# Sparse attention stage of a two-layer trunk: TensorE's order written out, attention as a three-step pipeline, index scores out of PSUM by ScalarE

## The chip, the core and the metric

The kernel runs on one NeuronCore of a Trainium2 chip. The core has five engines, each with its own in-order instruction queue: TensorE (PE, matrix products into PSUM; its weight loads are listed apart as PEld), VectorE (DVE), ScalarE (ACT), GpSimd (POOL) and SyncE (SP), which here only issues DMAs. Engines meet through semaphores. The metric is the device time of one execution in microseconds (us); the kernel before takes 1209.16 us, the median of three runs (1204.34 to 1213.13).

## The reference

A trunk of two layers on 512 tokens of width 1024. Layer 0 mixes tokens by sparse attention whose keys an indexer chooses, layer 1 by a gated linear attention; beside either, four heads attend to 256 memory rows. Each layer ends in a mixture of 32 experts. What the change touches lies wholly in layer 0's mixer:

```python
def dsa_mixer(x, cos, sin, w_in, idx_k_g, idx_k_b):
    q, k, v, qi, ki, wi, qm = _split(x @ w_in, DSA_SPLITS)   # 768 768 768 512 64 8 256
    q, k, qi = (rope of each, 12, 12 and 8 heads of 64)
    ki = apply_rope(layer_norm(ki, idx_k_g, idx_k_b), cos, sin)
    wi = wi * (IDX_HEADS ** -0.5 * IDX_DIM ** -0.5)
    out = sparse_attention(q, k, v, qi, ki, wi, topk)        # topk = 128
    return out.reshape(B, S, SEQ_WIDTH), qm

def block(args):                                             # of sparse_attention
    rel = jax.nn.relu(jnp.einsum('bqhd,bsd->bqhs', qib, ki))
    score = jnp.einsum('bqhs,bqh->bqs', rel, wib)            # 8 index heads, weighted
    score = jnp.where(causal[None], score, -jnp.inf)
    _, sel = lax.top_k(score, topk)
    ...                                                      # softmax over the chosen keys, times v
```

`memory_attention` is a plain softmax attention of the 256 columns `qm` over keys and values `mem @ w_kv`.

## The kernel before

Tokens lie in four blocks of 128 partitions (`NT` = 4). A projection of f32 accuracy is made of three fast matmuls (`mm3`, L340 to L342): each operand is split into a high part (L295, ScalarE) and the rest (L296, VectorE). `in_proj` (L558) makes one projection of 384 columns: for each token block 8 x 3 matmuls into one of two PSUM buffers (`mm`), then what `consume` does with the result. For keys and queries that is `rope` (ScalarE copies the result out, L467; VectorE multiplies, L452 and L455; GpSimd adds, L456), later three transposes by TensorE (L463) and a copy; for values a copy alone. Keys, queries and values come in two halves of six heads, in the order keys, queries, values.

**The indexer** (L594): for the query blocks 1 to 3 (block 0 needs no choice), eight heads' scores over 256, 384 or 512 keys. Each head is one matmul (L606) into one of two PSUM buffers (`sc`); VectorE takes it out with relu and the head's weight in one operation (L609 for head 0, L612 for the others), and GpSimd adds it to the sum (L613). Then 16 steps choose 8 keys each: MAX8 (L621) and MATCH_REPLACE (L622) on VectorE; at the end a mask is written (L624). The function is a generator: each head and each step of the choice is one `yield`.

**Attention** (`attend`, L527): a generator with one `yield` for a query block of a pair of heads. It holds two scores (L535), the softmax of both (`softmax_rows`: mask-add with row maximum L497, or the maximum alone L501 for memory, negation L503, exp on ScalarE L504, reciprocal L506, scaling L507), transposes (L463) with copies by ScalarE (L467) and the products with the values (L545), two heads of 64 columns side by side. There are 8 such items for memory and 24 for the six pairs of heads, with one to four key blocks. `put_mixed` (L515) splits a finished pair for the output projection.

**What sets the order.** `dsa_layer` draws steps from these generators between the token blocks of the projections: `KVC` steps of the indexer between the parts of the memory keys, and by `IS` so many steps of indexer, memory attention and `early` (the first three pairs of heads) after each token block. The scheduler of the framework may then reorder instructions of each engine, TensorE's too: it places each by when its inputs are expected. The last three pairs run between the parts of the second layer's memory keys (`mem_kv(1)`). Weights are loaded by SP's DMAs; `clear` writes zeros to the experts' output from a GpSimd memset, by DMAs in ScalarE's queue.

Of the kernel before, what the change touches and what calls it, by code (L numbers as in the profile page):

```python
# [40 lines left out]
KVC = 6  # L41
IS = ((6, 0, 0), (7, 0, 0), (5, 1, 0), (0, 1, 0), (0, 0, 1), (0, 0, 2))
# [177 lines left out]

def run(steps, n=None):

    r = None
    for r in itertools.islice(steps, n):
        pass
    return r


class Trunk:
# [105 lines left out]
    def mm3(self, ps, a, b):  # L335

        for k in range(KD):
# [4 lines left out]
            self.nc.tensor.matmul(ps, al, bh, start=False, stop=(k == KD - 1))  # L342

# [126 lines left out]
    def mem_kv(self, layer):  # L470
# [5 lines left out]
        for half, dst in enumerate((kmT, vm)):  # L476
            w = self.split_pieces(wv[:, :, half * 256:(half + 1) * 256], 256)
            a, b = (m, w) if half else (w, m)
            for j in range(2):
                ps = self.mm([P, 512])  # L480
                self.mm3(ps[:, :NMEM], lambda k: self.piece(a, k, j * P, (j + 1) * P), lambda k: self.piece(b, k))
# [36 lines left out]
    def attend_start(self):  # L518
        self.pr, self.pt = Ring(self.ar, 512, 3), Ring(self.ar, 512, 4)
# [30 lines left out]

    def mem_attention(self, qmT, kmT, vm, mix):
# [6 lines left out]
    def in_proj(self, wview, c0, n, x, consume, between=None, w=None, lags=(LAG,) * NT):  # L558
        w = w or self.split_pieces(wview[:, :, c0:c0 + n], n)
        for i in range(NT):  # L560
            ps = self.mm([P, 512])
            self.mm3(ps[:, :n], lambda k: self.piece(x, k, i * P, (i + 1) * P), lambda k: self.piece(w, k))
# [31 lines left out]
    def indexer(self, qiT, kiT, wi, bias, acc_b):  # L594

        nc = self.nc
# [3 lines left out]
        for i in range(1, NT):  # L600
            n = (i + 1) * P
            acc = acc_b.v(n, at=(0, 0, 2, 5)[i] * P)
            for h in range(IDX_H):
                j, s = divmod(h, 2)
                ps = self.sc([P, 512])
                nc.tensor.matmul(ps[:, :n], qiT[s * HD:(s + 1) * HD, j, i * P:(i + 1) * P],  # L606
                                 kiT[s * HD:(s + 1) * HD, :n], start=True, stop=True)
# [7 lines left out]
            nc.gpsimd.tensor_scalar(acc, acc, 0.0, 1.0, op0=OP.add, op1=OP.mult)  # L615
# [19 lines left out]
    def dsa_layer(self, Y):  # L635
# [85 lines left out]
        for kv_b, kmT, vm in self.mem_kv(0):  # L721
            run(choice, KVC)
# [1086 lines left out]
```

## Time and profile before

| | us |
|---|---|
| median of three runs | 1209.16 |
| lowest, highest | 1204.34, 1213.13 |
| profiled execution | 1212.06 |
| its span, first to last instruction | 1210.3 |
| TensorE busy in the span | 1105.9 |
| VectorE, ScalarE busy | 591.2, 398.5 |

The mean granted TensorE clock is 0.939 of full speed. The sparse attention stage fills about the first 330 us; behind it come the output projection with a layer norm and the router, to about 405, and the first experts' stage, to about 650; the second layer has the rest. A busy time is an average over stages with different limits, so the rows below are of single stretches. The clock column (PEclk) is the mean of the granted clock over a window: 1.00 is the higher of its two levels, 0.50 the lower.

### The profile page before, as it was taken

The numbers are of one execution on the slowest core, as the hardware profiler recorded it, in microseconds if no ns is written. First come the engines' busy times: TensorE is split into PE (matmuls) and PEld (weight loads), VectorE is DVE, ScalarE is ACT, GpSimd is POOL, SyncE is SP. The second block draws the span as 40 slices with busy tenths as digits, with TensorE's granted clock in tenths as the row PEclk, the third lists the DMA queues.
The fourth block names the chain that finished last, engine by engine and source line by source line (L and its number), as shares of the span: only waits on it lengthen the run. The fifth ranks groups of instructions, "written<-read, shape, count | busy, mean of one in ns | idle before, by whom it ended". The sixth has DMA issues, their size and how long they took to land. (4 is left out here: it accounts for less than half of the span.)

```text
span 1210.3 us, 20344 instructions
## 1 busy us (share of the span) xinstructions
PE 1105.9 (91%) x7864; PEld 799.5 (66%) x7864; DVE 591.2 (49%) x1601; ACT 398.5 (33%) x853; POOL 178.8 (15%) x179
## 2 busy tenths in 40 slices
PE   7999999999998899888988999899896999888985
PEld 7866887767697656444444778899896666444442
DVE  6778894555647422114116745992737322114125
ACT  6421343556512222112215534453501222112212
POOL 0425201000002021111000000553001111111000
PEclk9988899999998899998899999899997999998988
DMA  9033410341577699999997202137196899999992
GB/s 320 27 105 109 131 40 14 101 145 32 189 289 270 253 395 419 422 366 384 396 407 257 79 22 80 41 117 267 65 413 243 317 400 397 368 368 392 408 410 109
DMA packets 101509, 289.35 MB, mean 239 GB/s; under 512 B 13948, under 2 KB 43021, under 8 KB 89762
## 3 DMA queue, kind: packets, MB, share of 16 engines
q1 hardware_dynamic: 88704, 257.42, 56.4%
q0 software_dynamic: 9792, 20.00, 4.5%
q10 hardware_dynamic: 2914, 10.61, 2.2%
q8 instruction: 63, 1.03, 0.4%
q14 instruction: 36, 0.29, 0.1%
HBM read 272.19 MB, written 31.46 MB: 251 GB/s over the span
## 5 line engine op out<-in xcount | busy, mean ns | idle before, releaser
L1103 PE MATMUL mm<-blk,blk 128*64 128x256 f32 x2048 | 246.8, 391 | 30.9 <-DMA blk<-in_w 28.9
L340 PE MATMUL mm<-blk,blk 128*128 128x256 f32 (+2 forms) x800 | 262.7, 329 | 4.6 <-ACT blk L467 3.6
L341 PE MATMUL mm<-blk,blk 128*128 128x256 f32 (+2 forms) x800 | 256.3, 320 | 2.1 <-DVE blk L296 2.1
L342 PE MATMUL mm<-blk,blk 128*128 128x256 f32 (+2 forms) x800 | 255.8, 320 | 0.0
L1103 PEld LDWEIGHTS mm<-blk,blk 128*64 128x64 f32 x2048 | 149.9, 141 | 127.9 <-DMA blk<-in_w 43.0
L340 PEld LDWEIGHTS mm<-blk,blk 128*128 128x128 f32 x800 | 154.8, 194 | 25.7 <-issue 16.5
L1107 DVE TENSOR_TENSOR sa<-sa,mm 128x128 f32<-128x128 f32 x64 | 18.3, 287 | 304.9 <-ACT sa L1106 304.9
L341 PEld LDWEIGHTS mm<-blk,blk 128*128 128x128 f32 x800 | 155.1, 194 | 9.7 <-issue 7.2
L342 PEld LDWEIGHTS mm<-blk,blk 128*128 128x128 f32 x800 | 154.7, 193 | 7.9 <-issue 7.9
L1266 PE MATMUL pv<-blk,aT 128*64 128x512 f32 x512 | 129.7, 638 | 5.4 <-DMA blk<-in_w 2.5
L296 DVE TENSOR_TENSOR blk<-blk,blk 128x768 fp32r<-128x768 f32 (+3 forms) x104 | 106.8, 1041 | 37.3 <-ACT blk L295 37.1
L295 ACT ACTIVATE blk<-blk 128x768 fp32r<-128x768 f32 (+3 forms) x104 | 84.6, 835 | 73.2 <-DMA blk<-in_dsa_w_in 18.2
L1106 ACT ACTIVATE sa<-mm 128x128 f32<-128x128 f32 x64 | 17.7, 277 | 246.5 <-PE mm L1103 246.5
L1266 PEld LDWEIGHTS pv<-blk,aT 128*64 128x64 f32 x512 | 40.0, 146 | 85.4 <-issue 61.9
L1170 POOL DMA_INDIRECT blk<-x1d,at x32 | 34.1, 1065 | 303.0 <-DVE at L1136 232.0
L467 ACT ACTIVATE blk<-tr 128x256 f32<-128x256 f32 (+5 forms) x148 | 57.3, 404 | 53.8 <-PE tr L463 50.2
L1274 ACT ACTIVATE ys<-pv,wts 128x512 f32<-128x512 f32 x56 | 38.5, 687 | 81.1 <-PE pv L1266 56.0
L463 PE MATMUL tr<-cpack,blk 128*128 128x128 f32 x292 | 50.6, 285 | 6.2 <-DVE blk L1439 2.4
L463 PEld LDWEIGHTS tr<-cpack,blk 128*128 128x128 f32 x292 | 34.0, 143 | 19.0 <-issue 7.8
L545 PE MATMUL pv<-blk,blk 128*64 128x128 f32 x368 | 45.3, 289 | 0.3 <-ACT blk L467 0.2
L456 POOL TENSOR_TENSOR rope<-rope,rope 128x384 f32<-128x384 f32 (+2 forms) x28 | 26.1, 933 | 126.8 <-DVE rope L455 112.1
L1282 POOL DMA_INDIRECT Y<-ys,at x28 | 28.3, 1011 | 99.5 <-ACT ys L1274 96.4
(289 smaller groups left out, 1421.4 us busy)
## 6 DMA issues: line engine op xcount, KB each, us to landing
blk<-in_w SPq DMA_DIRECT2D x91, 1024.0 KB
blk<-in_w SPq DMA_DIRECT2D x112, 512.0 KB
blk<-in_w SPq DMA_DIRECT2D x147, 256.0 KB
blk<-in_dsa_w_in SPq DMA_DIRECT2D x24, 384.0 KB
blk<-in_gla_w_in SPq DMA_DIRECT2D x24, 384.0 KB
blk<-in_w SPq DMA_DIRECT2D x11, 768.0 KB
Y<-blk ACTq DMA_DIRECT2D x8, 1024.0 KB
blk<-in_w_out SPq DMA_DIRECT2D x16, 512.0 KB
```

Source lines behind the costliest of these rows:

```text
L295: self.nc.scalar.activation(hi, raw, AF.Copy)
L296: (eng or self.nc.vector).tensor_sub(lo, raw, hi.bitcast(F32))
L340: self.nc.tensor.matmul(ps, ah, bh, start=(k == 0), stop=False)
L341: self.nc.tensor.matmul(ps, ah, bl, start=False, stop=False)
L342: self.nc.tensor.matmul(ps, al, bh, start=False, stop=(k == KD - 1))
L463: self.nc.tensor.transpose(t[:s.shape[-1], j, :], s, self.ident)
L467: self.nc.scalar.activation(dst, src, AF.Copy)
L545: nc.tensor.matmul(o[s * HD:(s + 1) * HD, i * P:(i + 1) * P], vcol(j, s), pts[s][:, j, :], start=(j == 0), stop=(j == nk - 1))
L1103: nc.tensor.matmul(h[c * CAP:(c + 1) * CAP, 0:256], xe[k][:, e4 * CAP:(e4 + 1) * CAP], w[:, c * 256:(c + 1) * 256], start=(k == 0), stop=( ...
L1170: self.nc.gpsimd.indirect_dma_start(out=xs[j], out_offset=None, in_=self.x1d, in_offset=bass.IndirectOffsetOnAxis(ap=at[:, j:j + 1], axis= ...
L1266: nc.tensor.matmul(y[h * CAP:(h + 1) * CAP, :], aT[:, s + h, f * CAP:(f + 1) * CAP], ws[h][1][2 * f + c], start=(f == 0), stop=(f == 1))
L1274: nc.scalar.activation(ys[:, cs], y, AF.Copy, scale=wt[:, j:j + 1])
```

## The change

Four things change in `dsa_layer` and what it calls; nothing of the rest.

- `indexer` returns two generators, `scores` and `choice`. A step of `scores` is now two heads: two matmuls next to each other, then for each head two ACTIVATEs on ScalarE (Relu out of PSUM, then a Copy with the head's weight as scale, in SBUF) in place of VectorE's one operation. GpSimd's adds stay.
- `attend` is replaced for this layer by `pipeline`: each item has three steps, `first` (two scores and the softmax), `second` (transposes and their copies) and `third` (products with the values), and the steps of three items that follow each other alternate.
- `Weave` draws from such generators inside a projection, after each eighth of a token block (three matmuls, a *tick*), by a rate: 0.17 steps of scores and 0.3 of choice a tick, later 0.9 and 1.2 steps of the pipeline.
- All of it stands under `pe_order()`, which makes TensorE run in the order in which the program is written. The ring of softmax results has four places instead of three, and transposes of keys and queries follow three token blocks behind instead of two.

```diff
-KVC = 6
-IS = ((6, 0, 0), (7, 0, 0), (5, 1, 0), (0, 1, 0), (0, 0, 1), (0, 0, 2))
+PACE = (0.17, 0.3, 0.9, 1.2)
...
+    def __call__(self):
+        for s in self.streams:
+            s[2] += s[1]
+            while s[2] >= 1:
+                s[2] -= 1
+                next(s[0], None)
...
-        self.pr, self.pt = Ring(self.ar, 512, 3), Ring(self.ar, 512, 4)
+        self.pr, self.pt = Ring(self.ar, 512, 4), Ring(self.ar, 512, 4)
...
+        for n in range(len(items) + 2):
+            for f, m in ((first, n), (second, n - 1), (third, n - 2)):
+                if 0 <= m < len(items):
+                    f(m)
+                    yield
...
-                if h == 0:
-                    nc.vector.tensor_scalar(acc, ps[:, :n], 0.0, wi[:, i, h:h + 1], op0=OP.max, op1=OP.mult)
-                else:
-                    t = self.wk.tile([P, 512], F32, name="sct", tag="smask")
-                    nc.vector.tensor_scalar(t[:, :n], ps[:, :n], 0.0, wi[:, i, h:h + 1], op0=OP.max, op1=OP.mult)
-                    nc.gpsimd.tensor_add(acc, acc, t[:, :n])
-                yield
...
+                    pss = [self.sc([P, 512]) for _ in range(2)]
+                    for s, ps in enumerate(pss):
+                        nc.tensor.matmul(ps[:, :n], qiT[s * HD:(s + 1) * HD, j, i * P:(i + 1) * P],
+                                         kiT[s * HD:(s + 1) * HD, :n], start=True, stop=True)
+                    for s, ps in enumerate(pss):
+                        h = 2 * j + s
+                        t = self.wk.tile([P, 512], F32, name="sct", tag="smask")[:, :n] if h else acc[i]
+                        nc.scalar.activation(t, ps[:, :n], AF.Relu)
+                        nc.scalar.activation(t, t, AF.Copy, scale=wi[:, i, h:h + 1])
+                        if h:
+                            nc.gpsimd.tensor_add(acc[i], acc[i], t)
...
-        for kv_b, kmT, vm in self.mem_kv(0):
-            run(choice, KVC)
+        order = self.pe_order()
+        order.__enter__()
+        both = Weave((scores, PACE[0]), (choice, PACE[1]))
+        kv_b, kmT, vm = run(self.mem_kv(0, both))
...
+        for c in (1, 0, 2):
+            project(c, 0, both)
+        for quarter in range(2):
+            self.clear(Y, quarter)
+        project(1, 1, both)
+        run(scores)
...
+        early = itertools.islice(pipe, 3 * 20 - 3)
+        project(0, 1, Weave((choice, PACE[1]), (early, PACE[2])))
+        run(choice)
...
+        project(2, 1, Weave((early, PACE[2])))
...
+        self.kv = run(self.mem_kv(1, Weave((pipe, PACE[3]))))
+        run(pipe)
```

The first place is TensorE's order among the index scores of query block 2 (before L606, after L674; L340 to L342 and L353 to L355 are a projection's matmuls). Before:

```order
L606 MATMUL sc<-blk_288,blk_287 128x384
L342 MATMUL mm<-blk_1005,blk_102 128x384
L340 MATMUL mm<-blk_1005,blk_101 128x384
L606 MATMUL sc<-blk_288,blk_287 128x384
L341 MATMUL mm<-blk_1006,blk_101 128x384
L606 MATMUL sc<-blk_288,blk_287 128x384
L342 MATMUL mm<-blk_1005,blk_102 128x384
L340 MATMUL mm<-blk_1011,blk_113 128x384
L606 MATMUL sc<-blk_288,blk_287 128x384
```

and of the change:

```order
L354 MATMUL mm<-blk_979,blk_89 128x384
L355 MATMUL mm<-blk_978,blk_90 128x384
L674 MATMUL sc<-blk_288,blk_287 128x384 x2
L353 MATMUL mm<-blk_984,blk_101 128x384
L354 MATMUL mm<-blk_985,blk_101 128x384
L355 MATMUL mm<-blk_984,blk_102 128x384
L353 MATMUL mm<-blk_984,blk_101 128x384
```

Single heads between one or two matmuls of a projection have become two heads together, with 18 matmuls to the next two.

The second place is TensorE's order among the items beside the second layer's memory keys (before L535, L463, L545 for scores, transposes and products with values; after L576, L478, L599). Before:

```order
L535 MATMUL sc<-blk_988,blk_989 128x384
L463 MATMUL tr<-cpack,blk_1591 128x128 x2
L535 MATMUL sc<-blk_988,blk_989 128x384
L535 MATMUL sc<-blk_988,blk_989 128x512
L545 MATMUL pv<-blk_1672,blk_990 64x128
L545 MATMUL pv<-blk_1658,blk_990 64x128
L545 MATMUL pv<-blk_1672,blk_990 64x128
L340 MATMUL mm<-blk_3195,blk_2945 128x256
```

and of the change, without a row left out:

```order
L576 MATMUL sc<-blk_967,blk_968 128x128 x2
L353 MATMUL mm<-blk_2938,blk_2957 128x256
L354 MATMUL mm<-blk_2939,blk_2957 128x256
L355 MATMUL mm<-blk_2938,blk_2958 128x256
L478 MATMUL tr<-cpack,blk_1885 128x128 x4
L478 MATMUL tr<-cpack,blk_1895 128x128 x4
L353 MATMUL mm<-blk_2938,blk_2957 128x256
L354 MATMUL mm<-blk_2939,blk_2957 128x256
L355 MATMUL mm<-blk_2938,blk_2958 128x256
L599 MATMUL pv<-blk_1914,blk_969 64x128
L599 MATMUL pv<-blk_1919,blk_969 64x128
L599 MATMUL pv<-blk_1914,blk_969 64x128
```

Scores of two items and products of one head have become whole steps, each with both heads, and three matmuls between two steps.

The third place is VectorE's order near the end of the choice. Before, among the scores of query block 3 (L621 and L622 are a step of the choice for block 2, L609 and L612 take scores out of PSUM):

```order
L622 MATCH_REPLACE blk_795<-m_1174,blk_795 128x384
L455 TENSOR_TENSOR rope_1300<-rope_1297,blk_282 128x6x32
L621 MAX m_1177<-blk_795 128x8
L455 TENSOR_TENSOR rope_1300<-rope_1297,blk_282 128x6x32
L622 MATCH_REPLACE blk_795<-m_1177,blk_795 128x384
L609 TENSOR_SCALAR blk_795<-sc,wi 128x512
L621 MAX m_1180<-blk_795 128x8
L612 TENSOR_SCALAR sct<-sc,wi 128x512
```

and of the change, at the end of the choice for block 3 (L696, L697 a step, L699 the mask; L309 a split, L467 and L470 rope of the second half's keys, L516 and L518 the first memory item's maxima):

```order
L309 TENSOR_TENSOR blk_1844<-blk_1841,blk_1843 128x768
L467 TENSOR_TENSOR rope_1692<-rope_1690,blk_282 128x384
L470 TENSOR_TENSOR rope_1693<-rope_1690,blk_282 128x6x32 x2
L697 MATCH_REPLACE blk_732<-m_2232,blk_732 128x512
L699 TENSOR_SCALAR blk_290<-blk_732 128x512
L467 TENSOR_TENSOR rope_1734<-rope_1732,blk_282 128x384
L470 TENSOR_TENSOR rope_1735<-rope_1732,blk_282 128x6x32 x2
L467 TENSOR_TENSOR rope_1773<-rope_1771,blk_282 128x384
L470 TENSOR_TENSOR rope_1774<-rope_1771,blk_282 128x6x32 x2
L309 TENSOR_TENSOR blk_2392<-blk_2389,blk_2391 128x768
L467 TENSOR_TENSOR rope_1812<-rope_1810,blk_282 128x384
L470 TENSOR_TENSOR rope_1813<-rope_1810,blk_282 128x6x32 x2
```

No operation that empties PSUM stands between the steps of the choice any more, and the rope tiles of the second half's keys stand at its end; the first memory item's maxima (L516) come right behind these rows.

## Rows read from the trace of the kernel before

**Rows 1.** Windows of TensorE alone: stretch, its length, busy time with the number of records, mean granted clock, DMA share, GB/s.

```profile
55.00:142.00 87.00, 82.30 (x361) 0.82 0.37 120
142.00:330.00 188.00, 185.77 (x1116) 0.98 0.24 78
```

**Rows 2.** Timeline of TensorE from 73 to 78 us: start, duration, engine, line, operation, records that follow each other; in brackets the idle time before and what ended it.

```profile
73.46 0.34 PE L342 MATMUL mm<-blk,blk 128*128 128x384 f32 x1
...
75.22 0.34 PE L340 MATMUL mm<-blk,blk 128*128 128x384 f32 x1
75.39 0.33 PE L341 MATMUL mm<-blk,blk 128*128 128x384 f32 x1
77.97 0.91 PE L606 MATMUL sc<-blk,blk 64*128 64x384 f32 x2 [2.25 <-DVE blk L609]
```

**Rows 3.** The same view at the first index score of query block 3.

```profile
109.28 1.12 PE L606 MATMUL sc<-blk,blk 64*128 64x512 f32 x2 [2.31 <-DVE blk L609]
```

**Rows 4.** TensorE's groups by form in 55 to 330 us: count, then busy time and mean ns of one, then idle time before.

```profile
L340 PE MATMUL mm<-blk,blk 128*128 128x384 f32 x192 | 71.6, 373 | 0.0
...
L463 PE MATMUL tr<-cpack,blk 128*128 128x128 f32 x152 | 29.0, 288 | 1.5 <-DVE blk L507 0.8 <-DVE rs L506 0.6
...
L463 PE MATMUL tr<-cpack,rope 128*128 128x128 f32 x48 | 8.5, 285 | 0.0
```

**Rows 5.** Timeline of TensorE from 289 to 329 us, rows of scores (sc), products with values (pv) and transposes (tr); a score or product leaves two records.

```profile
289.71 1.12 PE L535 MATMUL sc<-blk,blk 64*128 64x512 f32 x2
290.77 0.55 PE L463 MATMUL tr<-cpack,blk 128*128 128x128 f32 x3
...
300.82 0.27 PE L463 MATMUL tr<-cpack,blk 128*128 128x128 f32 x1
...
311.00 0.43 PE L545 MATMUL pv<-blk,blk 128*64 128x128 f32 x2
311.36 0.70 PE L535 MATMUL sc<-blk,blk 64*128 64x256 f32 x2
311.99 0.55 PE L463 MATMUL tr<-cpack,blk 128*128 128x128 f32 x3
...
320.57 1.27 PE L535 MATMUL sc<-blk,blk 64*128 64x512 f32 x4
...
326.51 0.60 PE L463 MATMUL tr<-cpack,blk 128*128 128x128 f32 x4
...
328.07 1.09 PE L545 MATMUL pv<-blk,blk 128*64 128x128 f32 x14
```

**Rows 6.** VectorE's groups by form in 67.5 to 175 us.

```profile
L296 DVE TENSOR_TENSOR blk<-blk,blk 128x768 fp32r<-128x768 f32 x15 | 16.6, 1103 | 0.0
L621 DVE MAX8 m<-blk 128x8 f32<-128x512 f32 x16 | 11.1, 691 | 0.0
L622 DVE MATCH_REPLACE8 blk<-m,blk 128x512 f32<-128x512 f32 x16 | 10.9, 680 | 0.0
L621 DVE MAX8 m<-blk 128x8 f32<-128x384 f32 x16 | 8.8, 550 | 0.0
...
L621 DVE MAX8 m<-blk 128x8 f32<-128x256 f32 x15 | 6.3, 421 | 0.1
L455 DVE TENSOR_TENSOR rope<-rope,blk 128x192 f32<-128x192 f32 x18 | 6.2, 344 | 0.0
...
L452 DVE TENSOR_TENSOR rope<-rope,blk 128x384 f32<-128x384 f32 x9 | 5.4, 599 | 5.3 <-ACT rope L467 5.3
L612 DVE TENSOR_SCALAR sct<-sc,wi 128x512 f32<-128x512 f32 x7 | 5.2, 745 | 6.2 <-PE sc L606 5.0 <-POOL blk L613 1.1
```

**Rows 7.** VectorE's groups by form in 45 to 330 us, those of the softmax and of the largest split.

```profile
L506 DVE RECIPROCAL rs<-smx 128x1 f32<-128x1 f32 x64 | 10.1, 160 | 15.1 <-ACT blk L504 14.5
...
L503 DVE TENSOR_SCALAR nm<-mx 128x1 f32<-128x1 f32 x64 | 8.7, 145 | 0.2
...
L497 DVE CUSTOM_DVE_ANT_0 smask<-sc,blk 128x512 f32<-128x512 f32 x12 | 8.1, 683 | 1.0 <-PE sc L535 1.0
...
L296 DVE TENSOR_TENSOR blk<-blk,blk 128x1024 fp32r<-128x1024 f32 x6 | 7.3, 1221 | 2.1 <-ACT blk L295 2.1
...
L507 DVE TENSOR_SCALAR blk<-blk,rs 128x512 f32<-128x512 f32 x12 | 5.8, 485 | 0.4
...
L497 DVE DVE_READ_ACCUMULATOR2_ANT mx<- 128x1 f32 x48 | 4.0, 83 | 0.0
L507 DVE TENSOR_SCALAR blk<-blk,rs 128x128 f32<-128x128 f32 x12 | 3.4, 283 | 0.1
...
L497 DVE CUSTOM_DVE_ANT_0 smask<-sc,blk 128x128 f32<-128x128 f32 x12 | 3.2, 286 | 5.4 <-PE sc L535 5.4
```

**Rows 8.** ScalarE's groups by form in 45 to 330 us.

```profile
L504 ACT ACTIVATION_READ_ACCUMULATOR blk<-smask,nm 128x1 f32 x48 | 9.0, 188 | 0.0
L504 ACT ACTIVATE blk<-smask,nm 128x512 f32<-128x512 f32 x12 | 8.6, 718 | 5.0 <-DVE nm L503 4.9
...
L467 ACT ACTIVATE blk<-tr 128x512 f32<-128x512 f32 x12 | 7.0, 595 | 7.2 <-PE tr L463 7.2
```

**Rows 9.** Timeline of SP's DMA queue near the end of attention: the first issues of the experts' weights.

```profile
303.89 28.34 SPq L1055 DMA_DIRECT2D blk<-in_w  x11
```

**Rows 10.** Window of the first experts' stage: stretch, its length, busy time of PE, PEld, DVE, ACT and POOL, granted clock, DMA share, GB/s.

```profile
405.00:650.00 245.00, 224.45 (x1514) 125.97 (x1511) 61.96 (x177) 53.20 (x107) 27.18 (x29) 0.97 0.99 392
```

More of the change, by code (lines that the diff above doesn't have):

```diff
@@ L333, in free_pieces, with mm3 @@
             lo.free()
[L335 removed]
+    def mm3(self, ps, a, b, tick=None):
         for k in range(KD):
@@ new lines, in choice @@
+        def choice():
+            for i in range(1, NT):
+                while i not in scored:
+                    yield
+                for _ in range(TOPK // 8):
+                    m8 = self.sm.tile([P, 8], F32, name="m8")
+                    nc.vector.max(m8, acc[i])
+                    nc.vector.match_replace(acc[i], m8, acc[i], TAKEN)
+                    yield
+                nc.vector.tensor_scalar(bias[i], acc[i], TAKEN_T, NEG, op0=OP.is_ge, op1=OP.mult)
+        return scores(), choice()
@@ L726, in pair @@
         def pair(hp):
-            return self.attend(hp, lambda s: qT[s * HD:(s + 1) * HD, hp, :], lambda s: kT[s * HD:(s + 1) * HD, hp, :],
-                               lambda j, s: v[:, j, (2 * hp + s) * HD:(2 * hp + s + 1) * HD], lambda i: i + 1, bias,
-                               mix, hp)
-        self.attend_start()
-        memory = self.mem_attention(qmT, kmT, vm, mix)
-        early = itertools.chain(*(pair(hp) for hp in range(3)))
-        def steps(c, m, e):
-            def f():
-                run(choice, c)
-                run(memory, m)
-                if e:
-                    run(choice)
-                    run(early, e)
-            return f
@@ L744, in dsa_layer @@
[L744 to L756 removed]
+            return [(i, lambda s: qT[s * HD:(s + 1) * HD, hp, :], lambda s: kT[s * HD:(s + 1) * HD, hp, :],
+                     lambda j, s: v[:, j, (2 * hp + s) * HD:(2 * hp + s + 1) * HD], i + 1, bias, mix, hp)
+                    for i in range(NT)]
@@ new lines, in project @@
+        def project(c, half, tick):
+            base, got = ((0, got_qk(qT, half)), (768, got_qk(kT, half)), (1536, got_v(half)))[c]
+            self.in_proj(wv, base + half * 384, 384, x, got, lags=(3,) * NT, tick=tick)
+        for c in (1, 0, 2):
[4 more added lines that the diff above has]
+        run(scores)
+        for b in (qiT_b, kiT_b):
+            b.free()
+        items = self.mem_items(qmT, kmT, vm, mix)
@@ new lines, in dsa_layer @@
+        for hp in range(6):
+            items += pair(hp)
+        self.attend_start()
+        pipe = self.pipeline(items)
+        early = itertools.islice(pipe, 3 * 20 - 3)
+        project(0, 1, Weave((choice, PACE[1]), (early, PACE[2])))
+        run(choice)
+        self.rope_b.free()
+        acc_b.free()
+        mix.alloc()
+        project(2, 1, Weave((early, PACE[2])))
+        self.finish()
+        for b in (qmT_b, kv_b):
+            b.free()
+        for quarter in range(2, 4):
+            self.clear(Y, quarter)
```

104 lines of the change are left out of this document (59 added, 45 removed).

## The prediction

> **What bounds the kernel now.** The change touches only the first layer's sparse attention stage, so I read the engine windows of that stretch first. [rows 1] are TensorE's: from the first index score (55 us) to the last P·V (330 us) its busy time is 268.1 of 275 us. TensorE bounds the stage, but it does not run at its best: in 55 to 142 the mean granted clock is 0.82 and 4.7 us are idle, in 142 to 330 it is 0.98 and 2.2 us are idle. At half speed a stretch does half the work, so the clock costs 87 x 0.18 = 15.7 and 188 x 0.02 = 3.8 us; with the idle time 26.4 us are in plain sight.
>
> The timeline of TensorE shows how that comes about. In [rows 2] it waits 2.25 us in front of an index score, and again 2.31 us at 109.28 in [rows 3], both times for VectorE's L609: two PSUM buffers hold scores, and the operation that empties one stands in VectorE's queue among the steps of the choice. Right behind each of these waits lies a stretch at the slow clock.
>
> The third thing to see is how the heads' matmuls lie. [rows 5]: one head's score of 512 columns, alone, takes 1.06 us to the next start (289.71 to 290.77); four records, which are two heads, take 1.27 with their tail against 1.12 for two. Two heads next to each other on TensorE share the time, since each uses one half of the array; apart, each pays in full. P·V is the same: 14 records take 1.09, 2 take 0.43, so 0.055 for one more record, 0.22 for a pair of heads, and 0.36 for a head alone (311.00 to 311.36).
>
> **TensorE's work, before and after.** Prices: a projection matmul of 384 columns 0.176 us (ten starts from 73.46 to 75.22 in [rows 2]), of 256 columns in proportion 0.117 (estimate); a transpose (0.60 - 0.27) / 3 = 0.11 [rows 5]; a score 1.06 for 512 and 0.63 for 256 columns (311.36 to 311.99), so on that line 0.845 for 384 and 0.415 for 128. A change between the score or P·V kind and the rest costs between nothing and 0.36 - 0.22 = 0.14; I take 0.1, nearer to the row.
> - Projections: 576 x 0.176 = 101.4 and 190 x 0.117 = 22.2; 200 transposes (152 + 48) 22.0 [rows 4]; router 0.9.
> - 44 pairs of scores (4 index pairs each of 256, 384, 512; 8 memory items of 256; 6 head pairs with 128 to 512), heads together: 10 x 1.06 + 10 x 0.845 + 18 x 0.63 + 6 x 0.415 = 32.9. 76 pairs of P·V x 0.22 = 16.7.
> - In the order before, 16 of the score pairs stand apart (5 of 512, 5 of 384, 4 of 256, 2 of 128) and 31 of the P·V pairs, with 208 changes of kind; after it none and none, with 150. I counted the whole listings of which the front shows pieces.
>
> After: 101.4 + 22.2 + 22.0 + 0.9 + 32.9 + 16.7 + 15.0 = 211.1 us without any wait. Before: apart 12.8 and 6.8 more, changes 20.8, so 236.5; the trace has 274.4, and the 38 us between are the 26.4 above and some 11.5 of short gaps.
>
> **What the change adds: waits.** TensorE's order is now fixed by hand, so each wait is its own.
> - VectorE up to the end of the choice. 24 evacuations of about 0.6 us (0.745 at 512 columns) leave it. What stays from about 67.5 us, where all but the first of its MAX8 begin [rows 6]: the steps of the choice 16 x (0.691 + 0.680) + 16 x 2 x 0.55 + 16 x 2 x 0.42 = 53 and 4 for the small loads between, 14 splits x 1.1 = 15.4, 9 rope tiles x 1.29 = 11.6, the last masks 2: 86, less about 2 for operations that overlap at their ends. That ends at 151. TensorE needs for the same part (128 triples of 384 columns 67.6, 9.1 of memory keys, index scores 10.1, 27 transposes 3.0, changes 2.3) 92 us, so stands at the second half's queries at 147, and wants there the transposes of the first rope tile that VectorE has behind the choice. Cost 5 us (0 to 12).
> - Index scores out by ScalarE: two ACTIVATEs a head, the nearest row 0.595 for 512 columns [rows 8], so 2.4 us a pair, beside 18 triples' matmuls of 3.2 and 1.2 of scores. With the splits and rope copies ScalarE is some nine tenths full there: 2 us (0 to 10). Its copy in SBUF is not in the trace; below by a free second pass, above by twice the row.
> - The first memory item finds its row maxima behind VectorE's last rope tiles, and the rest of the chain is still empty: 3 us (0 to 6).
> - The items. For four key blocks, from the scores' end to the last transposes: two heads' mask-add, read-out and negation on VectorE 2 x (0.683 + 0.083 + 0.145) = 1.8, the second exp with its read-out 0.9, reciprocal and scaling 0.65 [rows 7, 8], and five handings-over of some 0.1 (estimate): 3.8 us. Between the two stand three steps of other items and, at 0.9 steps a tick, 3.3 ticks of 0.53 = 1.75: with transposes 0.65, P·V 0.45, next scores 0.4 and changes 0.4 that is 3.6. So the 19 items there lose little, 3 us (0 to 10).
> - Beside the second layer's memory keys (1.2 steps a tick of 0.35) the cover is only some 2.8, in the bare tail less. And three engines run level: from where the weights of these keys can land (the last tile of the values) TensorE needs 5 + 34 + 8 = 47 by the prices above; VectorE 13.7 items x 2.45 (3.0 with four blocks, 1.9 with one) = 34, 6 splits x 1.22 and 8 of half that width, and the mixed rows 3: 49; ScalarE about the same. I take 9 us (4 to 25).
> - A fall of the clock behind one of these waits: 3 us (0 to 10).
>
> Sum of the waits: 5 + 2 + 3 + 3 + 9 + 3 = 25 (4 to 73). The stage's part is then 211 + 25 = 236 instead of 274.4: 38 us less. Y's clearing moves ahead of the second half's keys with its memsets on GpSimd and its DMAs in ScalarE's queue, both under an index score's adds: nothing, since GpSimd has some us to spare; without that cover 4 x 1 us. The fourth ring buffer costs only space. Loads of weights issued by SP keep their order.
>
> **Does it reach the end?** The expert weights' DMAs follow the end of attention (issues from 303.89 to 332, when attention's buffers come free [rows 9]), and the stage that they bound runs with a DMA share of 0.99 [rows 10]; as its stream is released by what the change makes earlier, it shifts whole. Blocks lie elsewhere and some transfers become smaller: +-5 us. The profiled run took 1212.06, 2.9 above the median, so 1212 - 38 = 1174 for it, and about 1171 for a median.
>
> **The rivals.**
> 1. *VectorE stays the bound of the first part* (choice, ropes and splits in one queue). For it: 86 us of work in 80 us. If splits take half as long again where GpSimd adds (14 x 0.55 = 8), and the clock is low for 24 us behind the wait (12), it is 20 us more: 1191. Against: 14.6 us leave its queue.
> 2. *ScalarE becomes the bound of the index scores.* If the SBUF pass takes 0.2 us more than its row, four ACTIVATEs and the copies exceed 4.4 us a pair; a wait of 1 us at 12 pairs, and slow clock of 8, make 20: 1191 too. The Trainium skill, "ScalarE: Activation LUTs", section Rules for kernel authors, says that relu and multiplication belong on VectorE, not ScalarE; by that rule the move costs time. The trace agrees in so far as one VectorE operation of 0.745 us [rows 6] becomes two of at least 0.595.
> 3. *Slower: the fixed order shows the softmax chain at every item.* VectorE may take the next item's mask-adds (1.8 us) and a split (1.1) ahead of this item's reciprocal and scaling; the chain is then 6.7 instead of 3.8, and 32 items x 2.9 = 93 us of waits with the 13 of the other terms end at 211 + 106 = 317, 43 us over the trace: about 1252. It loses by over 1% from W = 75, that is from 1.9 us an item. Against it: most items have fewer blocks, and rows of VectorE's new order show reciprocals between the maxima.
> 4. *The gain is lost in the experts' stage*, if that stream waits for something that doesn't move: 1209. Against: the issues of [rows 9] end with attention.
>
> **How the numbers follow.** The forecast 0.62 (1158 to 1186), rival 1 0.12, rival 2 0.10, rival 3 0.07, rival 4 0.06, and 0.03 for more than the forecast. About 1% (12 us) is what a measurement of this kernel can tell from no change. Of rivals 1 and 2 seven in ten still gain over 12 us; so faster 0.80, within 1% 0.13, slower 0.07. The range leaves the waits' far ends out: 1155 (waits of 9) to 1200 (waits of 54).
>
> **What would show it.** Right: attention's last P·V near 292 us, mean clock over 0.95 in the first part, no wait of scores for VectorE, single-head scores gone from the timeline, and idle rows of TensorE near the second half's queries and in the last 50 us. The step on heads is wrong if pairs that stand together still take twice; the step on the first part if queries start after 160 us; the items if TensorE's idle time behind 190 us is over 30 us. The whole is wrong if attention ends 38 us earlier and the experts' stage does not.

## The result and the profile after

The changed kernel takes 1178.89 us (1176.43 to 1179.51, three runs) instead of 1209.16: ratio 0.975, 95% interval 0.971 to 0.979. A second measurement, beside the later experiments, gave 0.974 (0.971 to 0.976). The profiled execution of the change took 1178.89 us with a span of 1177.1. That of before took 1212.06, and beside the experiments single executions of the kernel before lie between 1200.88 and 1215.36. So differences to its one trace can be some us too large; those between the versions with the new order are firmer.

The stage itself is seen best at attention's last P·V. In the trace of before it starts at 328.9 us, in that of the change at 292.0: 36.9 us earlier, from a first index score at 55.1 in both. The two windows that answer to [rows 1], of TensorE alone (length, busy time, granted clock, DMA share, GB/s):

```profile
55.00:142.00 87.00, 87.00 (x496) 1.00 0.30 98
142.00:292.00 150.00, 135.55 (x966) 0.98 0.29 93
```

In the first window nothing is idle any more, the clock is at its higher level throughout, and TensorE puts 496 records where it had 361. That goes on up to the second half's queries at 149.6:

```profile
55.00:149.50 94.50, 94.50 (x538) 1.00 0.27 90
```

The idle time has moved into the second window, where before it was 2.2 us. What TensorE waits for there (us in total, times, longest; `tr` are transposes, L482 is ScalarE's copy, L518 the negated maximum, L522 the scaling of a softmax):

```profile
PE sc L576 <- ACT blk L519: 7.2, 1, 7.2
PE tr L478 <- ACT blk L482: 5.2, 3, 2.7
PE tr L478 <- DVE nm L518: 1.2, 4, 0.6
PE tr L478 <- DVE blk L522: 0.5, 2, 0.3
```

One wait of 7.2 us is half of it. The clock falls to its lower level during that wait, at 156.15 us, and stays there for 6.8 us; TensorE works in the last 3.6 of these, which costs 1.8 us. The two parts of that stretch:

```profile
156.15:159.37 3.22, 0.00 (x0) 0.50 0.00 0
159.37:162.98 3.61, 3.61 (x12) 0.50 0.00 0
```

In TensorE's timeline the wait stands between the scores of the first and of the second memory item:

```profile
150.78 0.70 PE L576 MATMUL sc<-blk,blk 64*128 64x256 f32 x4
...
151.86 0.33 PE L355 MATMUL mm<-blk,blk 128*128 128x384 f32 x1
159.37 1.67 PE L576 MATMUL sc<-blk,blk 64*128 64x256 f32 x4 [7.18 <-ACT blk L519]
```

The second item's scores need a PSUM buffer that the first item's exp (L519) has read. ScalarE's timeline shows why that exp comes late:

```profile
148.15 0.49 ACT L482 ACTIVATE rope<-mm 128x384 f32<-128x384 f32 x1 [6.73 <-DVE rope L470]
155.11 0.84 ACT L308 ACTIVATE blk<-blk 128x768 fp32r<-128x768 f32 x1 [6.46 <-DMA blk<-in_dsa_w_in]
155.86 0.47 ACT L482 ACTIVATE rope<-mm 128x384 f32<-128x384 f32 x1
156.23 0.48 ACT L482 ACTIVATE blk<-tr 128x384 f32<-128x384 f32 x1
156.60 0.84 ACT L308 ACTIVATE blk<-blk 128x768 fp32r<-128x768 f32 x1
157.46 1.28 ACT L519 ACT_TABLE_LOAD   x1
158.75 0.47 ACT L519 ACTIVATE blk<-sc,nm 128x256 f32<-128x256 f32 x1
```

It stands 6.5 us at a split (L308) of the weights of the second half's values, because their load has not landed. SP issued that load only behind another one that waits for the end of the choice (L699, which starts at 148.74); SP's issues, and the wait ahead of the first of them:

```profile
149.62 0.34 SPq L325 DMA_DIRECT2D blk<-in_memT  x1
150.09 0.88 SPq L325 DMA_DIRECT2D blk<-in_dsa_w_in  x2
```

```profile
SPq L325 <- DVE blk L699: 16.7, 1, 16.7
```

The same late load also holds VectorE. Its half of that split (L309) stands ahead of the last rope tile and of the first memory item's maxima, so the negated maxima (L518) that exp needs come only at 158.53:

```profile
155.98 0.96 DVE L309 TENSOR_TENSOR blk<-blk,blk 128x768 fp32r<-128x768 f32 x1 [3.51 <-ACT blk L308]
...
158.53 0.27 DVE L518 TENSOR_SCALAR nm<-mx 128x1 f32<-128x1 f32 x2
```

Exp starts at 158.75, so both queues let it go within 0.1 us of each other. In ScalarE's queue a table load of 1.28 us for exp stands directly ahead of it as well.

The new operations on ScalarE, and the evacuation's cost (groups by form; mean ns of one behind the busy time):

```profile
L680 ACT ACTIVATE sct<-sct,wi 128x512 f32<-128x512 f32 x7 | 5.0, 724 | 0.1
...
L679 ACT ACTIVATE sct<-sc 128x512 f32<-128x512 f32 x7 | 4.1, 598 | 9.8 <-POOL blk L682 6.9 <-POOL blk L706 2.9
```

The pass out of PSUM costs what its nearest row said ([rows 8], 0.595); the scaled copy within SBUF costs 0.724, a fifth more. One VectorE operation of 0.745 us has become 1.32 us of ScalarE.

### The profile page after: what moved, and what is told of

Read it like the earlier page. It is cut to its first block, busy times and chain, and to the rows that moved or that the text cites. A ratio compares the mean times of both kernels' runs of the same rounds, so it can differ in the third digit from the quotient of the medians.

```text
span 1177.1 us, 20316 instructions
## 1 busy us (share of the span) xinstructions
PE 1060.8 (90%) x7864; PEld 778.4 (66%) x7864; DVE 584.5 (50%) x1577; ACT 415.0 (35%) x901; POOL 176.6 (15%) x179
## 5 line engine op out<-in xcount | busy, mean ns | idle before, releaser
L353 PE MATMUL mm<-blk,blk 128*128 128x256 f32 (+2 forms) x800 | 265.5, 332 | 3.8 <-ACT blk L482 3.8
L355 PE MATMUL mm<-blk,blk 128*128 128x256 f32 (+2 forms) x800 | 251.2, 314 | 0.0
L353 PEld LDWEIGHTS mm<-blk,blk 128*128 128x128 f32 x800 | 153.8, 192 | 32.1 <-issue 26.6
L355 PEld LDWEIGHTS mm<-blk,blk 128*128 128x128 f32 x800 | 153.5, 192 | 1.4 <-issue 1.4
L309 DVE TENSOR_TENSOR blk<-blk,blk 128x768 fp32r<-128x768 f32 (+3 forms) x104 | 106.5, 1040 | 41.1 <-ACT blk L308 39.9
L308 ACT ACTIVATE blk<-blk 128x768 fp32r<-128x768 f32 (+3 forms) x104 | 84.2, 836 | 69.3 <-DMA blk<-in_dsa_w_in 19.8
L482 ACT ACTIVATE blk<-tr 128x256 f32<-128x256 f32 (+5 forms) x148 | 55.7, 402 | 36.8 <-PE tr L478 33.5
L478 PE MATMUL tr<-cpack,blk 128*128 128x128 f32 x292 | 47.2, 286 | 8.4 <-ACT blk L482 2.7
L478 PEld LDWEIGHTS tr<-cpack,blk 128*128 128x128 f32 x292 | 34.9, 145 | 14.4 <-issue 4.9
L1741 POOL TENSOR_TENSOR blk<-blk,blk 96x1024 f32<-96x1024 f32 x7 | 26.8, 3838 | 91.3 <-ACT blk L1740 85.8
```

Of the source, the lines that this page charges most:

```text
L308: self.nc.scalar.activation(hi, raw, AF.Copy)
L309: (eng or self.nc.vector).tensor_sub(lo, raw, hi.bitcast(F32))
L353: self.nc.tensor.matmul(ps, ah, bh, start=(k == 0), stop=False)
L478: self.nc.tensor.transpose(t[:s.shape[-1], j, :], s, self.ident)
L482: self.nc.scalar.activation(dst, src, AF.Copy)
```

## The experiments

All are compared by the last P·V of their trace, which excludes what varies in the rest of the program; the time of the whole stands beside it, and the ratio is to executions of the kernel before that ran beside that version (their medians lie between 1205.9 and 1210.8). Each version has one trace; the two of the change lie 0.4 us apart. Up to e7, "Theory A" is the prediction's: the gain comes from heads side by side, from a VectorE queue without evacuations and from the pipeline, and is given back in part as waits. From e8 on the theories are about the wait of 7.2 us.

| kernel | last P·V | median us | ratio to before (95%) |
|---|---|---|---|
| before | 328.9 | 1209.2 | |
| the change | 292.0 | 1178.9 | 0.975 (0.971 to 0.979) |
| e12, the change again | 292.4 | 1180.4 | 0.974 (0.971 to 0.976) |
| e1, VectorE evacuates | 299.0 | 1186.0 | 0.983 (0.979 to 0.987) |
| e2, before with ScalarE evacuating | 318.7 | 1200.9 | 0.996 (0.993 to 0.998) |
| e3, products by head | 295.9 | 1180.3 | 0.979 (0.975 to 0.984) |
| e4, index heads apart | 299.6 | 1186.4 | 0.982 (0.977 to 0.987) |
| e5, order free | 290.4 | 1176.4 | 0.975 (0.970 to 0.979) |
| e7, one item at a time | 404.0 | 1290.5 | one run |
| e8, values first | 295.8 | 1190.1 | 0.987 (0.982 to 0.991) |
| e9, weights reused | 287.4 | 1175.7 | one run |
| e10, loads ahead, ring of three | 399.2 | 1284.1 | 1.060 (1.058 to 1.062) |
| e11, the same, order free | 303.6 | 1184.4 | 0.977 (0.975 to 0.979) |
| e13, clearings earlier | 291.1 | 1178.8 | 0.974 (0.971 to 0.977) |

**e1: VectorE takes the scores out again.**

```diff
-                        nc.scalar.activation(t, ps[:, :n], AF.Relu)
-                        nc.scalar.activation(t, t, AF.Copy, scale=wi[:, i, h:h + 1])
+                        nc.vector.tensor_scalar(t, ps[:, :n], 0.0, wi[:, i, h:h + 1], op0=OP.max, op1=OP.mult)
```

> The changed kernel with one part undone: an index score leaves PSUM by VectorE's single operation again (24 of about 0.6 us), and ScalarE's 48 ACTIVATEs are gone. Theory A (the first part of the stage is bounded by VectorE's queue, so taking 14.6 us off it was worth time): the choice ends 10 to 15 us later, the second half's queries start near 160 instead of 149 us, some index scores wait for VectorE again, the whole takes 1187 to 1195 us instead of 1179. Theory B (the gain is the order's alone; where the scores leave doesn't matter): 1177 to 1182 us and queries still near 149. Theory C (the rule that relu and multiplication belong on VectorE): faster than 1177 us.

The choice's last mask moves from 148.7 to 166.7 us, and a score waits for VectorE again. VectorE's row of that mask, and TensorE's wait in 55 to 160 us:

```profile
166.69 0.42 DVE L698 TENSOR_SCALAR blk<-blk 128x512 f32<-128x512 f32 x1
```

```profile
PE sc L674 <- DVE sct L679: 1.9, 1, 1.9
```

The last P·V is 7.0 us later. Theory A holds in kind, not in its sizes: the choice ends 18 us later (10 to 15 were expected), the queries start at 154.3, not near 160, so TensorE did not wait for the end of the choice there, and the whole takes 1186.0 (1187 to 1195).

**e2: ScalarE's evacuation alone, in the kernel before.** The same exchange at L609 and L612.

> The kernel before with one part of the change alone: each index score leaves PSUM by ScalarE's two ACTIVATEs; order, items and steps are those of before. Theory A (waits for VectorE in front of the index scores and the slow clock behind them were a good half of the gain): no score waits for VectorE, the mean granted clock of 55 to 142 us rises from 0.82 to over 0.95, and the whole is 12 to 22 us faster than before. Theory B (the order alone): within 4 us of before, since single heads between matmuls still make TensorE change its kind of work.

The last P·V comes 10.2 us earlier than before, 12 to 22 were expected of the whole, where 5 are measured. TensorE in 55 to 142 us, its clock and what it waits for:

```profile
55.00:142.00 87.00, 81.01 (x405) 0.92 0.36 120
```

```profile
PE sc L606 <- ACT sct L613: 3.7, 4, 1.9
PE sc L606 <- ACT blk L609: 1.6, 3, 0.7
```

The waits for VectorE (4.6 us in the kernel before) have become 5.3 us of waits for ScalarE, though ScalarE is busy for only 47.1 of the 87 us, and nearly half of the slow clock has stayed. A likely reason is that in the old order single heads follow each other so closely that whichever engine empties the two buffers is late; that is argued, not shown. Neither theory's number was right. With e1 it makes a table of four: order and pipeline alone bring 29.9 us, ScalarE's evacuation alone 10.2, both 36.9. By the medians of the whole the first two are 19.9 and 4.9.

**e3: the products of one head behind each other.**

```diff
-            for j in range(nk):
-                for s in range(2):
+            for s in range(2):
+                for j in range(nk):
```

> The changed kernel with the two loops of the products with the values exchanged: first all key blocks of one head, then of the other, so that heads no longer alternate and only one product of each can share the time with the other head's. Theory A (heads side by side share TensorE's time, and TensorE bounds most of the items): 44 pairs lose their partner at 0.21 us, 9.3 us of TensorE's work more, and 5 to 9 us on the whole, 1184 to 1188 us; the records of the products in the timeline then stand 0.10 us apart. Theory B (the chain of softmax bounds the items, so TensorE's work is hidden): under 3 us.

TensorE's timeline, the same two products, of three and then four key blocks, in the change and then in e3:

```profile
212.32 0.88 PE L599 MATMUL pv<-blk,blk 128*64 128x128 f32 x12
...
216.47 1.09 PE L599 MATMUL pv<-blk,blk 128*64 128x128 f32 x16
```

```profile
212.46 1.15 PE L599 MATMUL pv<-blk,blk 128*64 128x128 f32 x12
...
216.88 1.58 PE L599 MATMUL pv<-blk,blk 128*64 128x128 f32 x16
```

Four key blocks cost 0.49 us more, three 0.27, two nothing; over six pairs of heads that is 4.6 us, half of the 9.3 that I had priced for this edit. The last P·V is 3.9 us later. So nearly all of TensorE's extra work reaches the end of the stage: among the items TensorE is the bound, as theory A has it; my price of the edit was double. The whole, 1180.3, cannot be told from the change's 1178.9 and 1180.4; 1184 to 1188 were expected.

**e4: the index heads apart.** One `yield` a head, `PACE[0]` 0.34 instead of 0.17.

> The changed kernel with a step of the index scores cut into two: one head a step, at twice the rate, so that the 24 heads stand alone, 9 matmuls apart. All else is the same. Theory A (heads together share the time): 12 scores pay in full, 4 x (0.63 + 0.84 + 1.06) = 10 us, and 24 changes of kind more 2 us; queries start near 160 instead of 149 us, less what VectorE's queue hides, so 6 to 12 us on the whole, 1185 to 1191 us. Theory B (VectorE bounds this part up to 149 us whatever TensorE does): under 3 us.

TensorE turns to the second half's queries at 158.33 us in e4 and at 149.56 in the change (timelines, the first matmul of either):

```profile
158.33 0.42 PE L353 MATMUL mm<-blk,blk 128*128 128x384 f32 x1
```

```profile
149.56 0.42 PE L353 MATMUL mm<-blk,blk 128*128 128x384 f32 x1
```

That is 8.8 us later. To count from the same place in the program I take the last group of four rope transposes ahead of the scores, in e4 and then in the change:

```profile
50.74 0.60 PE L478 MATMUL tr<-cpack,rope 128*128 128x128 f32 x4
```

```profile
51.31 0.60 PE L478 MATMUL tr<-cpack,rope 128*128 128x128 f32 x4
```

From there to the queries it is 107.6 us against 98.3, so 9.3 more, against a price of 12. (The first index score is no such place: at twice the rate it comes earlier in the program.) The last P·V is 7.6 later, the whole 1186.4, as theory A expected. This is the term of heads side by side with its changes of kind, and it is not hidden by VectorE.

**e5: the order left to the scheduler.** `pe_order()` is taken off.

> The changed kernel without the fixed order: the scheduler places TensorE's instructions, from the same program of pipeline steps. Read at the last P.V, which is 292.0 us with the fixed order. Its listing has 14 products and 5 scores apart from their partner and 24 changes of kind more, 5 us of TensorE's work by my prices. Theory A (the gain is in the steps as the program writes them; the fixed order only keeps pairs together): 295 to 299 us. Theory B (the fixed order itself carries the gain): over 305 us. Rival 3 of the prediction (the fixed order makes TensorE wait where a scheduler would fill in): under 289 us.

The scheduler ends 1.6 us earlier, at 290.4, and the whole is as fast. That lies in none of the three ranges, and nearest to the one of rival 3. It fills the gap at 152 us with projection matmuls; its wait there is

```profile
PE sc L576 <- ACT blk L519: 2.4, 1, 2.4
```

instead of 7.2, with another of 1.7 for a copy by ScalarE (L482) ahead of it. But the clock is at its lower level for longer: its mean over 142 to 175 us is 0.79, in the change 0.90, which are 13.7 and 6.8 us of half speed. So theory B is out: the steps as written carry the gain, without the 3 to 7 us that theory A had added for the free order. The fixed order does make TensorE wait at this one place, as rival 3 had it, but for the stage that is worth under 2 us, and fixing the order adds nothing that these runs can tell.

**e7: one item at a time.**

```diff
-        for n in range(len(items) + 2):
-            for f, m in ((first, n), (second, n - 1), (third, n - 2)):
-                if 0 <= m < len(items):
-                    f(m)
-                    yield
+        for n in range(len(items)):
+            for f in (first, second, third):
+                f(n)
+                yield
```

> The changed kernel with the three steps of an item behind each other (scores and softmax, transposes, products) and only then the next item; the number of steps and their rates are the same. Between an item's scores and its transposes there is now one step's share of projection, 0.6 us, in place of some 3.6. Theory A (the pipeline hides the softmax chain of 2.5 to 3.8 us): each of 32 items waits 2 to 3 us, part of it shared with the waits that are there, and the slow clock comes with it: last P.V at 345 to 390 us instead of 292. Theory B (the chain is short against VectorE's and ScalarE's sums, which are the bound): under 310 us.

The last P·V comes at 404.0 us, 112 later, beyond the upper end expected. Waits and window of TensorE in 142 to 404 us:

```profile
PE tr L478 <- DVE rs L521: 35.1, 17, 8.4
PE tr L478 <- ACT blk L519: 16.2, 10, 2.1
PE tr L478 <- DVE blk L522: 10.9, 15, 3.0
PE tr L478 <- ACT blk L482: 4.4, 2, 3.8
```

```profile
142.00:404.00 262.00, 194.12 (x980) 0.76 0.18 58
```

Some 67 us of waits for the softmax and the copies of the same item, 2 us an item, and the clock at 0.76 of full speed. This is rival 3's loss, and the pipeline is what avoids it.

**e8: values first in the second half.** `project(2, 1)` takes the place of `project(1, 1)`, keys and queries follow beside the items.

> The changed kernel with the second half's projections in another order: values beside the end of the choice, then keys and queries beside the first attention items, in place of keys, then queries and values. Values need no rope, so VectorE has 4 rope tiles (5 us) less ahead of the end of the choice and of the first memory item, and later 4 more. Theory A (VectorE's queue sets the end of the first part): choice ends 3 to 5 us earlier, the wait of 7.2 us at the second item shrinks to 2 to 5, last P.V at 285 to 290 us instead of 292. Theory B (what stalls there is the split of weights ahead of exp in ScalarE's queue, VectorE is not it): the wait stays over 5 us and P.V ends within 2 us of 292, or later where the rope tiles meet the items.

The choice ends 1.8 us earlier, yet the wait is still 5.4, and the last P·V comes at 295.8: theory B. ScalarE again stands at a split, here 8.3 us, and VectorE 6.5 us at its half of it. Behind 190 us the clock is worse, 0.93 instead of 1.00, and that costs more than the wait gave back. The whole is 11 us longer than the change, of which 7 lie outside this stage and were not explained. The window of 190 to 292 us, e8 and then the change:

```profile
190.00:292.00 102.00, 93.71 (x648) 0.93 0.30 100
```

```profile
190.00:292.00 102.00, 96.25 (x725) 1.00 0.38 124
```

**e9: no load in ScalarE's way.** The values are projected with the queries' weights, as the expectation says.

> The changed kernel where the second half's values are projected with the weights of its queries, which stay in SBUF: the load and the four splits of the values' weights are left out, so half of the values are not the reference's. In the trace of the change ScalarE stands 6.5 us at a split whose load was issued at 150.1 us and landed 5 us later, with the first exp of attention behind it. Theory A (this split, not VectorE, makes the 7.2 us wait and the slow clock behind it): the wait falls under 2.5 us, no slow clock at 156, last P.V at 281 to 285 us. Theory B (the rest of VectorE's queue, rope tiles and choice, makes it): the wait stays over 5 us, last P.V after 288.

The wait falls to 2.0 us, the last P·V to 287.4, less than expected; the clock still falls for 10.2 us, and another wait of 1.8 appears, because ScalarE now stands at a DMA of Y's clearing until GpSimd's memset for it is done. Most of the shorter wait is a later start: the first item's scores come 2.2 us later than in the change, and exp starts only 1.9 us earlier. The edit also takes the values' splits out of VectorE's queue, so this run alone can't tell the two queues apart.

**e10, e11: the same loads ahead, nothing left out; fixed and free order.**

```diff
-        self.pr, self.pt = Ring(self.ar, 512, 4), Ring(self.ar, 512, 4)
+        self.pr, self.pt = Ring(self.ar, 512, 3), Ring(self.ar, 512, 4)
...
-        for quarter in range(2, 4):
-            self.clear(Y, quarter)
         self.free_pieces(x)
         self.load_router(0)
         self.kv = run(self.mem_kv(1, Weave((pipe, PACE[3]))))
+        for quarter in range(2, 4):
+            self.clear(Y, quarter)
```

> The changed kernel with two edits that move only loads: the ring of softmax results has three places again, and the last two of Y's clearings come after the second layer's memory keys. By the listing the loads of the second half's values then stand in SP's queue ahead of a load that waits for the end of the choice, the first is released by a matmul at 145 instead of the choice's end at 149.5, and only its split stands ahead of the first exp in ScalarE's queue, the second behind the first two exps. Nothing is left out. Theory A (the 7.2 us wait and the slow clock behind it come from ScalarE standing at a split for a load that SP issued late): the first exp starts near 153 instead of 158.8 us, the wait falls to 1 to 3 us, the last P.V to 281 to 287 us. Theory B (VectorE's rope tiles and the choice set it, the split only stands in their shadow): the first exp stays after 156 us and the last P.V within 2 us of 292.

> The same two edits with TensorE's order left to the scheduler. The free order took the last P.V from 292.0 to 290.4 us and the visible idle time from 14.4 to 5.6 us, which says that it fills part of the same wait with matmuls of the projection. Theory A: with that wait gone a free order has little left to fill, so this run ends within 2 us of the run with the fixed order. If the fixed order costs by itself, it ends 3 us or more earlier.

The edit was a mistake, and a telling one: contrary to the expectation it does not only move loads. With three places the softmax of the next item is written, in program order, over a row that the transposes of this item still have to read; attention's output is then not the reference's, and every item's transposes wait for the next item's softmax. TensorE's waits in e10, 142 to 400 us:

```profile
PE tr L478 <- DVE blk L522: 65.4, 30, 3.2
PE sc L576 <- ACT blk L519: 4.2, 1, 4.2
```

30 waits of 2.2 us, and the last P·V at 399.2. The free order (e11) has 303.6, 96 us less, where e5 found 1.6 between the two orders with four places. With these waits in both runs e11 can't answer what it was to answer, and both of its theories fail. For the question that was asked only the time up to the first exp counts, which the ring can't touch: ScalarE's split is done at 149 us, and yet the first exp starts at 154.55, 5.0 us behind the first scores instead of 8.0, held by VectorE. The row of ScalarE's timeline in e10:

```profile
154.55 0.47 ACT L519 ACTIVATE blk<-sc,nm 128x256 f32<-128x256 f32 x1 [3.13 <-DVE nm L518]
```

**e13: the clearings earlier, with four places.** One edit:

```diff
-        for c in (1, 0, 2):
+        for c in (1, 0):
             project(c, 0, both)
         for quarter in range(2):
             self.clear(Y, quarter)
+        project(2, 0, both)
```

> The changed kernel with one edit: the first two clearings of Y stand one projection earlier, ahead of the first half's values; the ring keeps its four places and nothing is left out. By the listing the first load of the second half's values then waits only for a matmul at about 132 us, and the second split stands behind the first two exps, as in the run with the loads ahead, where the first exp started 5.0 us behind the first scores instead of 8.0 and waited 3.1 us for VectorE. Theory A (the 7.2 us wait is in part ScalarE's late split, in part VectorE's rope tiles): first exp at 154 to 156 us, wait 3.5 to 5 us, last P.V at 286 to 290 us instead of 292. Theory B (VectorE alone): exp after 157 us, P.V after 291. If the split were all of it: exp before 153, P.V before 285.

The second memory item's scores in TensorE's timeline of e13, and the first exp in ScalarE's:

```profile
157.96 1.31 PE L576 MATMUL sc<-blk,blk 64*128 64x256 f32 x4 [3.86 <-ACT blk L519]
```

```profile
157.34 0.47 ACT L519 ACTIVATE blk<-sc,nm 128x256 f32<-128x256 f32 x1 [3.13 <-DVE nm L518]
```

The wait is 3.9 us, as theory A said, and exp starts 4.6 us behind the scores. But the scores themselves start 1.9 us later, since the choice's last mask now starts at 150.5 and the queries at 151.5 (why was not traced). So exp and P·V, at 157.3 and 291.1, miss theory A's times and lie within theory B's. A measure that this shift touches less is the time from the choice's last mask to the first exp. It is 10.0 us in the change (148.74 to 158.75), and 6.85 both here (150.49 to 157.34) and in e10 (147.70 to 154.55), where exp waits for VectorE's negated maxima alone. VectorE's masks in the change and in e13:

```profile
148.74 0.75 DVE L699 TENSOR_SCALAR blk<-blk 128x512 f32<-128x512 f32 x1
```

```profile
150.49 0.43 DVE L699 TENSOR_SCALAR blk<-blk 128x512 f32<-128x512 f32 x1
```

So of the 7.2 us some 3.2 are the late load, through either queue, as VectorE's own 3.5 us in front of its half of the split also say; the other 4 are VectorE's queue (rope tiles, a split, the maxima). Taking the first part away does not make the stage faster by as much: the last P·V is 0.9 us earlier.

**e12: the change once more.**

> The changed kernel once more, on the same chip as the two runs beside it, as the measure for them: 1176 to 1182 us, last P.V at 291 to 293 us.

Both came as expected: 1180.4 us, last P·V at 292.4. No version beat the change clearly: e5 and e13 are within its measurement. The rates in `PACE` and the later place of the transposes of keys and queries were not varied by themselves (e4 alone doubles one rate, together with half steps).

## Why the prediction was right, and where its sizes were off

The forecast was 38 us for the stage, and 36.9 came. The mechanism is as forecast: TensorE bounds the stage before and after, it has less work when partners stand together, and waits give part of it back. That the sum fits so well is in part luck. From the first index score to the last P·V the change takes 236.9 us; 211.1 are TensorE's work by the prices, so 25.8 lie above them, and 25 were forecast, all as waits. But the visible waits are only 14.4 us, and the lower clock costs 1.8. The other 9.6 are work and short gaps that the prices leave out; they were not taken apart. The prediction had found some 11.5 us of such gaps in the kernel before, and put none into its sum for the change. So waits forecast 9 us too high and gaps left out cancel. Term by term:

- *TensorE's work, heads side by side.* Right in kind, its sizes somewhat high: e4 measures 9.3 us for the 12 index pairs with their changes of kind against 12, and e3 4.6 us for the products against the 9.3 of its expectation.
- *VectorE up to the end of the choice, 5 us, and index scores out by ScalarE, 2 us.* Neither came: TensorE is never idle from 55 us to the second half's queries, and that they start at 149.6 instead of 147.0 is work above the prices. The order of events is as described: VectorE is busy for 71.4 of the 74.5 us from 67.5 to 142, and its last mask comes at 148.7, just in time. ScalarE is busy for 47.2 of the 87 us up to 142, so about half and not nine tenths. Rivals 1 and 2 did not come about. e1 shows how late VectorE would have been: 18 us at the choice's end.
- *The first memory item, 3 us (0 to 6).* This is the step that was mis-sized most: 7.2. The sum had VectorE's rope tiles, which e10 and e13 leave as some 4 us, but not that the exp and the maxima both stand behind a split whose load SP issues late. The prediction had "Loads of weights issued by SP keep their order" and looked no further; that the load ahead of this one waits for the end of the choice was not in it.
- *The clock, 3 us.* 1.8: of 6.8 us at half speed 3.2 lie within that wait and cost nothing more.
- *The items, 12 us.* 7.3 of visible waits. I forecast that most would lie beside the second layer's memory keys; the larger ones lie earlier, beside queries and values (1.4, 2.7 and 1.1 us at 179, 202 and 211).
- *Rival 3* is real as a mechanism (e7, e10: over 100 us), and the three-step pipeline keeps it away. That the fourth ring place "costs only space" was too little said: without it e10 loses the pipeline, and attention's output is not the reference's.

The time of the whole, 1178.9, lies 8 us over the forecast of 1171. Most of the difference is outside the stage. The rest of the program, from the last P·V to the end, takes 885.1 us in the change (1177.1 - 292.0) and 885.3 in its second profile, but 881.4 before, so 3.7 us were given back there. And I had taken off 2.9 us because the profile of before lies that much over its median; the profile of the change is itself the median. 36.9 - 3.7 - 2.9 = 30.3, the difference of the medians. What takes the 3.7 us was not tried. Transfers of the experts' weights have other sizes (74 instead of 91 of 1024 KB), as the prediction allowed with +-5. e1, e4, e5, e7 and e13 have 884.2 to 886.1, e2, in the old order, 881.7; but e3, in the new order, has 881.0, so the cause stays open.

The Trainium skill's rule ("ScalarE: Activation LUTs", section Rules for kernel authors) that relu and multiplication belong on VectorE agrees with the trace on the single operation: 0.745 us against 0.598 + 0.724. It decides nothing here: e1 and e2 show the dearer form faster by 7.0 and 10.2 us at the stage's end. In e1, with the cheaper form, VectorE is busy for 72.4 of the 74.5 us from 67.5 to 142, ScalarE for 19.6.

## What to carry to other kernels

Two heads of 64 rows or columns should stand next to each other in the program: setting the index heads apart again cost 7.6 us at the stage's end (e4), as much as giving their evacuation back to VectorE (7.0, e1), and no row of idle time shows it. A softmax chain of some 4 us (in e7 4.1 from an item's scores at 396.96 to its transposes at 401.04) is hidden by writing items as steps of a pipeline, with as many ring places as steps in flight need; whether a scheduler or the author fixes the order then matters little (1.6 us, e5). When an operation's input is wanted early, look through every in-order queue that leads to it, ScalarE's and SP's too: a load that waits holds up all behind it, here two engines at once. And when a sum fits, compare its terms: work that the prices leave out can hide a wait that did not come.

## What was unexpected of the hardware

A scaled copy of 512 columns within SBUF takes ScalarE 0.724 us, the relu of the same size out of PSUM 0.598; they differ in the memory and in the scale per partition, which were not taken apart. And a longer wait did not mean a longer time at the lower clock level: with the wait of 7.2 us in the change went 6.8 us (from 156.15), with e5's waits of 1.7 and 2.4 us 13.7 (from 158.29), with the 3.9 us of e13 3.4 (from 158.82), and with the wait of 2.7 us at 202 in the change none.
